# Searched priorities for three build-time schedules, a form for the sample transposes, other planned costs, and the last attention evacuations behind all products

## The chip, the cores and the metric

One core of a Trainium2 chip. Its engines run their own instruction queues and meet at semaphores: TensorE (PE; PEld is its weight load), VectorE (DVE), ScalarE (ACT), GpSimd (POOL) and SyncE (SP), which issues most DMAs. The metric is device microseconds of one execution, and what is given is the median of several runs.

## The reference

A two-layer trunk, one inference step. There are 512 new tokens of one prompt (`x_prompt`) and 8 x 4 = 32 tokens of 8 running sequences (`x_sample`), 544 rows of width 1024 in all.

```python
for i in range(DEPTH):
    h = rms_norm(x, norm_mix[i])
    if i % 2 == 0:    # conv: a*sigmoid(gate), causal depthwise conv of 31, layer norm, silu, w_out
        out, st = conformer_conv(h, conv_past[c], ...)
    else:             # stick-breaking attention, 16 heads of 64
        qkv = (h @ attn_w_qkv[a]).reshape(b, t, 3, N_HEADS, HEAD_DIM)
        att = stick_breaking_attention(q, k_all, v_all, attn_b_logit[a], past_len)
        out = att.reshape(b, t, N_HEADS * HEAD_DIM) @ attn_w_o[a]
    x = x + out
    h = rms_norm(x, norm_ffn[i])
    out, st = conv_ffn(h, ...)    # (silu(conv3(h @ w_gate)) * (h @ w_up)) @ w_down
    x = x + out
y = rms_norm(x, norm_final)
```

For the samples the keys and values of 256 past positions come from a paged cache, 2 pages of 128 rows for each sequence. The weights of attention are `exp(log_sigmoid(z) + sum over later keys of log_sigmoid(-z))`, a reversed running sum along the keys in place of a softmax. New K and V rows and the conv states are outputs too. Everything is f32.

## The kernel before, in words

**Numbers.** Each f32 product is made of three passes over split operands: x as XH + XL, a weight as whi + wlo, and XH·whi + XL·whi + XH·wlo. ScalarE makes whi from the raw weights (L397, a cast), VectorE wlo (L400, raw minus whi); a weight slot is 128 x 1024, and five split slots are in use in turn. The same holds for activations: XH by ScalarE, XL by VectorE.

**Stages, in order of time.** Conv mixer of layer 0 (to about 214.6 us): the rows come in as `xr` (128 rows each) and `xs` (the 32 sample rows), are transposed on TensorE (L998) and split to XH and XL (L1005, L1007); products with w_in at L755 to L757; depthwise taps as products of diagonals (L892); layer norm; w_out. FFN of layer 0 (to about 635): gate and up at L1401 to L1403, down at L1625 to L1627; the first products of the attention's queries lie in its end. Attention (to about 871): K and V products by 128 columns, called chunk c, at L2125 to L2127; K and V back to rows (L2155) for the outputs; pages gathered by POOL (`xT<-in_cache_k_dram`), turned (L2245) and used for sample logits (L2263, 32 columns at a time) and sample values (L2325, 32 rows); prompt logits with 64 contracted rows (L2387); exp, ln, running sum and exp on ScalarE and VectorE; the weights transposed (L2429) and multiplied by V into 64 columns (L2449, tile `av`). For chunks 0 to 6 `av` is copied whole; for chunk 7, the last, three units of products go to `av`, and each 128-column block of it is cast to XH (L2458) and subtracted to XL (L2459). Then w_o and, with an order of its own, the FFN of layer 1 and the final norm (to 1268).

**What sets the order.** No order is written out by hand. Each stage makes a list of operations of `Plan` (class at L105) with an engine, a planned cost in us, what they read and write, and the function that issues the instructions. `run` then walks planned time: for the engine that is free first it takes, among the operations whose inputs are ready about then, the one with the smallest key, and calls its function, so that all queues are filled in that order:

```python
t + CHANGE_BIAS * turn - self.eager * rank[i] - self.urgent.get(i, 0.0) -
    (STICK if self.follows.get(i, -1) == last.get(eng) else 0.0)
```

`rank` is the longest planned chain behind the operation. `urgent` holds written urgencies plus the **shifts**, a string of `index:delta` pairs, where index counts the operations of the list in the order of their making. `turn` is 0.17 us (times CHANGE_BIAS, 3) if a TensorE operation has another `form` than the one before it; None is the form of the plain 128 x 128 matmuls, "c32", "c64" and "r64" are blocks with 32 or 64 output columns or 64 contracted rows. PSUM and other buffers are handed out in the order in which operations come to use them. The conv list is `Plan(E_CONV, 0.12, CONV_SHIFTS)` (L718), FFN `Plan(E_FFN)` (L1311), attention `Plan()` (L2077). Planned costs and arrival times serve the order alone; on the chip an engine waits for what its instruction needs.

Of the kernel before, what the change touches and what calls it, by code (L numbers as in the profile page):

```python
# [14 lines left out]
ALU = mybir.AluOpType  # L15
# [234 lines left out]
def tile_trunk(  # L250
# [737 lines left out]
    def incoming(h):  # L988
# [3 lines left out]
        for j in range(NC // per):  # L992
            pt = psum(("tr", "av")[(j + 1) % 2])
            for i in range(per):
                c = j * per + i
                o = i * n
                for t, m, b in mine:
                    plan.op("pe", 0.107, lambda c=c, o=o, t=t, m=m, b=b, pt=pt: pe.transpose(  # L998
                        pt()[:, o + b * P - c0:o + b * P - c0 + m], t[:, c * P:(c + 1) * P], ident[:m, :m]),
                        r=[("x", b)], w=[pt])  # L1000
# [300 lines left out]
    def ffn(l, before, after):  # L1301
# [9 lines left out]
        plan = Plan(E_FFN)  # L1311
# [765 lines left out]
    plan = Plan()  # L2077
# [22 lines left out]
    def dcost(n):  # L2100
        return 0.09 + n * 1.1e-3

    def acost(n):
        return 0.1 + n * 0.95e-3
# [55 lines left out]
    def keys(c, h):  # L2160
        c0, n = (SA, SB)[h]
        pt = project(k0 + TURNS.index(("k", c)), h)
        plan.op("act", acost(256), lambda: act.copy(kT[:, c, c0:c0 + 256], pt()[:, :256]),  # L2163
                r=[pt], w=[("k", c, h)] + ([("ktp", i) for i in range(4)] if c >= 4 else []))
        if h:
            plan.op("act", 0.2, lambda: act.copy(kT_s[:, c, :], pt()[:, 256:n]), r=[pt], w=[("kT_s", c)])
        rows, src = to_rows(lambda b: kT[:, c, c0 + b * P:c0 + (b + 1) * P], [("k", c, h)])
        kr = sbuf("kr", 2 * P, 2)
        plan.op("dve", 0.38, lambda: dve.tensor_copy(kr().rearrange("p (b d) -> p b d", b=2), src()), r=[rows], w=[kr])
        plan.op("sp", 3.0, lambda: nc.sync.dma_start(out=kpv[:, 2 * h:2 * h + 2, c * P:(c + 1) * P],  # L2170
                                                     in_=kr().rearrange("p (b d) -> p b d", b=2)), r=[kr])

    def values(c, h):
# [4 lines left out]
        if h:  # L2178
            plan.op("act", 0.2, lambda: act.copy(vT_s[:, c, :], pt()[:, 256:n]), r=[pt], w=[("vT_s", c)])
        rows, src = to_rows(lambda b: vt()[:, b * P:(b + 1) * P], [vt])  # L2180
        plan.op("dve", 0.38, lambda: dve.tensor_copy(vtok[c % 3][:, 2 * h:2 * h + 2, :], src()),
# [23 lines left out]
    def page(i):  # L2205
# [21 lines left out]
    def page_logits(m):  # L2227
# [8 lines left out]
        for odd in range(2):  # L2236
            for pg in range(2):
                t = page(4 * m + 2 * odd + pg)
                for half in range(2):
# [7 lines left out]
                    plan.op("pe", 0.43, turn, r=[t, (t, 1), "pages"], w=[pt])  # L2247
# [6 lines left out]
                    plan.op(eng, 0.68 if half == 0 else 0.6, keep, r=[pt], w=[("ktq" if odd else "ktp", 2 * pg + half)],  # L2254
# [11 lines left out]
        plan.op("pe", 1.72, logits, r=[(k, i) for k in ("ktp", "ktq") for i in range(4)] + ["Qz", *second], w=[z], form="c32")  # L2266
        if m % 2:
            for g in range(2):
                plan.op("dve", 0.45, lambda g=g: dve.tensor_scalar(
# [3 lines left out]
    def new_logits():  # L2273
# [10 lines left out]
        plan.op("pe", 0.6, f, r=[("kT_s", c) for c in range(NC)], w=[zn], form="c32")  # L2284
        for t in range(4):
            plan.op("dve", 0.25, lambda t=t: dve.scalar_tensor_tensor(
# [3 lines left out]
    def to_columns(t, pt, src, dst, key, r):  # L2290

        plan.op("pe", 0.12, lambda: [pe.transpose(pt()[:, i * P:(i + 1) * P], x, ident) for i, x in enumerate(src)], r=r, w=[pt])
        plan.op("act", 0.12 + 0.12 * len(src), lambda: act.copy(dst, pt()[:, :len(src) * P].rearrange("p (g r) -> p g r", r=P)),
# [10 lines left out]
    def new_weights():  # L2304
# [3 lines left out]
        for i in range(4):  # L2308
            rows = slice(32 * i, 32 * i + 32)
            plan.op("act", 0.2, lambda rows=rows: act.activation(Zw[rows, :, rows], Zn[rows], AF.Exp), r=["Zn"], w=[("Zw", i)])  # L2310
# [3 lines left out]
    def sequence(n):  # L2314
# [13 lines left out]
        plan.op("pe", 0.9, f, r=[*ts, *((t, 1) for t in ts), ("wT", 2 * bg), ("wT", 2 * bg + 1), "pages"], w=[pt], form="c32")  # L2328
# [4 lines left out]
        else:  # L2333
            plan.op("dve", 0.37, lambda: dve.scalar_tensor_tensor(o, pt()[:, :2 * P], m, o, op0=ALU.mult, op1=ALU.add),
# [4 lines left out]
    def new_values(bg):  # L2339
# [19 lines left out]
        plan.op("act", 0.4, lambda: act.copy(  # L2359
# [9 lines left out]
    def pair(c):  # L2369
        av = psum("av")  # L2370

        def unit(parts):
# [17 lines left out]
            plan.op("pe", 1.69e-3 * n, logits, r=[x for cc in cs for x in (("q", cc), ("k", cc, 0), ("k", cc, 1))], w=z, form="r64")  # L2390
            for j in range(2):
                for cc, (lo, m) in cs.items():
                    plan.op("act", acost(m), lambda j=j, cc=cc, lo=lo, m=m: act.activation(
# [12 lines left out]
            plan.op("dve", 0.1 + n * 1.06e-3, lambda: dve.tensor_scalar(  # L2406
# [4 lines left out]
            for j in range(2):  # L2411
                for i, lo, _ in parts:
# [6 lines left out]
                    plan.op("dve", 0.08 + m * 2.15e-3, scan, w=[(s, j)])  # L2419
            sj = [(s, 0), (s, 1)]  # L2420
            plan.op("act", acost(2 * n), lambda: act.activation(two(s)[:, :, :n], two(s)[:, :, :n], AF.Exp, scale=-1.0), w=sj)
            plan.op("dve", 0.08 + 2 * n * 1.08e-3, lambda: dve.tensor_tensor(
                two(e)[:, :, :n], two(e)[:, :, :n], two(s)[:, :, :n], op=ALU.mult), r=sj, w=ej)
            for j in range(2):
# [6 lines left out]
                plan.op("pe", 0.82e-3 * n, turn, r=[(e, j)], w=[t])  # L2431
# [148 lines left out]
```

## Time and profile before

| | us |
|---|---|
| median of 3 runs | 1270.52 (1269.94 to 1270.71) |
| profiled execution | 1269.8 |
| span of its trace | 1268.1 |
| TensorE busy | 1257.2, 10846 matmuls |
| VectorE busy | 1004.7, 1696 instructions |
| ScalarE busy | 717.5, 1436 instructions |
| GpSimd busy | 166.0, 291 instructions |
| granted clock of TensorE | 0.998 of full speed |

A row of the timeline is: start, duration, engine, line, operation, out<-in, tile or shape, count, and in brackets the idle time before it with what ended it. A row of the waits is: engine, tile and line that waited, what it waited for, then total us, times and longest. A row of the groups is: line, engine, operation, shapes, count, then busy us and mean ns, then idle time before. A row of the windows is: stretch of time, sum of busy time of all engines that count, then busy us of PE, PEld, DVE, ACT and POOL with their counts, the granted clock, the share of DMA and GB/s. Matmuls are pipelined, so a row's duration overlaps the next row's start; the spacing of starts is what one costs.

### The profile page before, as it was taken

The numbers are of one execution on the slowest core, as the hardware profiler recorded it, in microseconds if no ns is written. First come the engines' busy times: TensorE is split into PE (matmuls) and PEld (weight loads), VectorE is DVE, ScalarE is ACT, GpSimd is POOL, SyncE is SP. The second block draws the span as 40 slices with busy tenths as digits, with TensorE's granted clock in tenths as the row PEclk, the third lists the DMA queues.
The fourth block names the chain that finished last, engine by engine and source line by source line (L and its number), as shares of the span: only waits on it lengthen the run. The fifth ranks groups of instructions, "written<-read, shape, count | busy, mean of one in ns | idle before, by whom it ended". The sixth has DMA issues, their size and how long they took to land.

```text
span 1268.1 us, 26470 instructions
## 1 busy us (share of the span) xinstructions
PE 1257.2 (99%) x10846; PEld 1207.7 (95%) x10846; DVE 1004.7 (79%) x1696; ACT 717.5 (57%) x1436; POOL 166.0 (13%) x291
## 2 busy tenths in 40 slices
PE   9999999999999999999999999999999999999998
PEld 8997699999999999999989888999999999999998
DVE  7999876979987887869865589766988987886863
ACT  7794584635655455445564598754646645455453
POOL 5000014101001000002042143200111001000000
PEclk9999999999999999999999999999999999999999
DMA  7455423133233233244354443342123233232221
GB/s 221 131 165 156 119 69 115 35 100 102 92 112 99 74 112 115 62 144 172 116 185 154 152 144 132 119 145 73 62 85 117 91 96 117 67 119 91 85 77 72
DMA packets 119179, 142.39 MB, mean 112 GB/s; under 512 B 5101, under 2 KB 110245, under 8 KB 118786
## 3 DMA queue, kind: packets, MB, share of 16 engines
q1 hardware_dynamic: 110350, 111.89, 28.2%
q0 software_dynamic: 8704, 28.80, 7.0%
q8 instruction: 85, 1.39, 0.5%
q14 instruction: 36, 0.29, 0.1%
q10 hardware_dynamic: 4, 0.01, 0.0%
HBM read 129.34 MB, written 12.18 MB: 112 GB/s over the span
## 4 chain that ended last, share of the span: by engine, by line
PE 88%; DVE 9%; ACT 1%; issue 1%; DMA 0%; DVEq 0%; ACTq 0%
PE acc L1627 5%; PE acc L1626 5%; PE acc L1625 5%; PE acc L755 4%; PE acc L756 4%; PE acc L757 4%; PE av L892 3%; PE tr L1627 3%; PE tr L1626 3%; PE tr L1625 3%; PE av L1401 3%; PE av L1402 3%; PE av L1403 3%; PE tr L1401 3%; PE tr L1402 3%; PE tr L1403 3%
## 5 line engine op out<-in xcount | busy, mean ns | idle before, releaser
L397 ACT CAST whi<-raw 128x1024 fp32r<-128x1024 f32 (+2 forms) x247 | 224.3, 912 | 122.2 <-PE av L1402 25.1
L400 DVE TENSOR_TENSOR wlo<-raw,whi 128x1024 fp32r<-128x1024 f32 (+2 forms) x247 | 259.1, 1052 | 26.6 <-ACT whi L397 24.9
L755 PE MATMUL acc<-XH,whi 128*128 128x288 f32 (+1 forms) x384 | 112.7, 294 | 0.0
L757 PE MATMUL acc<-XH,wlo 128*128 128x288 f32 (+1 forms) x384 | 110.3, 287 | 0.9 <-DVE wlo L400 0.9
L756 PE MATMUL acc<-XL,whi 128*128 128x288 f32 (+1 forms) x384 | 110.3, 287 | 0.0
L1401 PE MATMUL av<-HH,whi 128*128 128x288 f32 (+1 forms) x280 | 83.3, 298 | 0.4 <-DVE xT L1716 0.4
L1627 PE MATMUL acc<-TH,wlo 128*128 128x272 f32 x288 | 83.0, 288 | 0.0
L1626 PE MATMUL acc<-TL,whi 128*128 128x272 f32 x288 | 82.7, 287 | 0.0
L1625 PE MATMUL acc<-TH,whi 128*128 128x272 f32 x288 | 82.7, 287 | 0.0
L1402 PE MATMUL av<-HL,whi 128*128 128x288 f32 (+1 forms) x280 | 82.6, 295 | 0.0
L2125 PE MATMUL acc<-XH,whi 128*128 128x256 f32 (+1 forms) x264 | 82.0, 311 | 0.6 <-ACT kT L2163 0.6
L1403 PE MATMUL av<-HH,wlo 128*128 128x288 f32 (+1 forms) x280 | 82.3, 294 | 0.0
L1661 ACT COPY G<-acc 128x272 f32<-128x272 f32 (+1 forms) x72 | 26.8, 372 | 94.7 <-PE acc L1627 94.7
L1401 PE MATMUL tr<-HH,whi 128*128 128x256 f32 (+1 forms) x280 | 79.1, 283 | 0.0
L1402 PE MATMUL tr<-HL,whi 128*128 128x256 f32 (+1 forms) x280 | 78.9, 282 | 0.0
L1403 PE MATMUL tr<-HH,wlo 128*128 128x256 f32 (+1 forms) x280 | 78.5, 280 | 0.0
L2127 PE MATMUL acc<-XH,wlo 128*128 128x256 f32 (+1 forms) x264 | 75.8, 287 | 0.0
L2126 PE MATMUL acc<-XL,whi 128*128 128x256 f32 (+1 forms) x264 | 75.8, 287 | 0.0
L755 PEld LDWEIGHTS acc<-XH,whi 128*128 128x128 f32 x384 | 72.2, 188 | 1.4 <-issue 0.4
L757 PEld LDWEIGHTS acc<-XH,wlo 128*128 128x128 f32 x384 | 72.1, 188 | 1.1 <-DVE wlo L400 1.1
L756 PEld LDWEIGHTS acc<-XL,whi 128*128 128x128 f32 x384 | 72.2, 188 | 0.3
L1564 DVE SCALAR_TENSOR_TENSOR cv<-G,fprm,cv 128x560 f32<-128x560 f32 x88 | 69.5, 797 | 0.5
(465 smaller groups left out, 4372.7 us busy)
## 6 DMA issues: line engine op xcount, KB each, us to landing
raw<-in_ffn_w_gate_dram SPq DMA_DIRECT2D x22, 1024.0 KB
raw<-in_ffn_w_up_dram SPq DMA_DIRECT2D x22, 1024.0 KB
raw<-in_ffn_w_down_dram SPq DMA_DIRECT2D x24, 768.0 KB
raw<-in_attn_w_qkv_dram SPq DMA_DIRECT2D x12, 1024.0 KB
raw<-in_conv_w_in_dram POOLq DMA_DIRECT2D x6, 1024.0 KB, 8.7
rep<-glu SPq DMA_DIRECT2D x36, 142.0 KB
raw<-in_conv_w_out_dram POOLq DMA_DIRECT2D x4, 1024.0 KB, 7.0
raw<-in_ffn_w_down_dram SPq DMA_DIRECT2D x8, 512.0 KB
```

What stands on the lines that cost most here:

```text
L397: act.copy(hi[:, k, :], src[:, k])
L400: dve.tensor_tensor(lo[:, k, :], src[:, k], hi[:, k, :], op=ALU.subtract)
L755: pe.matmul(o, hi[:, k, :], XH[:, k, c0:c0 + n], start=(k == 0), stop=False)
L756: pe.matmul(o, hi[:, k, :], XL[:, k, c0:c0 + n], start=False, stop=False)
L757: pe.matmul(o, lo[:, k, :], XH[:, k, c0:c0 + n], start=False, stop=(k == NC - 1))
L1401: pe.matmul(o, hi[:, j + k, :], xh, start=(start and k == 0), stop=False, **kw)
L1402: pe.matmul(o, hi[:, j + k, :], xl, start=False, stop=False, **kw)
L1403: pe.matmul(o, lo[:, j + k, :], xh, start=False, stop=(stop and k == len(xs) - 1), **kw)
L1625: pe.matmul(o, hi[:, j + k, :], xh, start=(start and k == 0), stop=False, **kw)
L1626: pe.matmul(o, hi[:, j + k, :], xl, start=False, stop=False, **kw)
L1627: pe.matmul(o, lo[:, j + k, :], xh, start=False, stop=(k == 3), **kw)
L2125: pe.matmul(o, hi[:, k, :], XH[:, k, c0:c0 + n], start=(k == 0), stop=False)
```

## The change

Every product, copy and DMA stays; both kernels issue the same instructions. Five edits concern their order.

1. `CONV_SHIFTS` becomes another table of searched numbers.
2. The attention list gets such a table (`ATTN_SHIFTS`), and the FFN list gets one for layer 0 (`FFN_SHIFTS`); layer 1's has none, as before.
3. Transposes of the 32 sample rows in the conv stage have a form, "x32", so leaving and entering them is charged as a turn.
4. Many planned costs of the attention list are other numbers, and a page counts as there 5.6 us after its gather in place of 4.0.
5. For the last chunk, the casts and subtractions of `av` read all three units of products, where each had read its own.

```diff
 CONV_SHIFTS = (
-    "14:-0.3 19:-5.6 22:-0.9 26:-9.4 28:-1.2 30:-9.6 31:-6.4 37:-7.1 40:-29.6 41:-19.9 42:-3.6 46:-3.3 47:-6.6 49:-12.8 51:-6.1 "
...
+    "18:-4.8 19:2 22:-3.9 26:-6.9 32:-13 36:-14.1 38:-3.4 39:-9 40:-0.8 42:-3.2 43:-0.8 47:-6.8 48:-11.2 50:-4.7 52:-5.3 53:-3.9 "
...
+ATTN_SHIFTS = (
+    "9:0.4 10:6.7 21:19 29:4.8 35:4.5 41:5 49:2.8 50:-5.6 53:-22.8 96:-1.7 115:0.3 124:2.4 130:7.9 136:4.4 146:2.2 174:-0.2 175:-6.9 "
...
+FFN_SHIFTS = (
+    "11:0.6 13:-10.2 17:-13.3 34:-2.8 35:2.4 37:2.8 38:0.7 41:-0.4 48:-7.5 49:-6.8 55:-1.6 56:-7.6 58:7.5 60:3.2 64:-13 101:-17.8 "
...
                         pt()[:, o + b * P - c0:o + b * P - c0 + m], t[:, c * P:(c + 1) * P], ident[:m, :m]),
-                        r=[("x", b)], w=[pt])
+                        r=[("x", b)], w=[pt], form="x32" if m < P else None)
...
-        plan = Plan(E_FFN)
+        plan = Plan(E_FFN, shifts="" if l else FFN_SHIFTS)
...
-    plan = Plan()
+    plan = Plan(shifts=ATTN_SHIFTS)
     plan.change = CHANGE
...
     def dcost(n):
-        return 0.09 + n * 1.1e-3
+        return 0.05 + n * 1.045e-3
 
     def acost(n):
-        return 0.1 + n * 0.95e-3
+        return 0.035 + n * 0.9e-3
...
-            plan.op(f"page{i}", 4.0, lambda: None, r=[("asked", i)], w=[(t, 1)])
+            plan.op(f"page{i}", 5.6, lambda: None, r=[("asked", i)], w=[(t, 1)])
...
-        plan.op("pe", 1.72, logits, r=[...], w=[z], form="c32")
+        plan.op("pe", 1.695, logits, r=[...], w=[z], form="c32")
...
-            products(range(len(units)), 2.1, av)
+            products(range(len(units)), 2.165, av)
...
             for u in range(len(units)):
                 for i, _ in units[u]:
-                    out(i * P, P, lambda cols: av()[:, cols], [(av, u)], i)
+                    out(i * P, P, lambda cols: av()[:, cols], [(av, v) for v in range(len(units))], i)
```

The lines of the changed kernel are 27 higher than those of the same code before, from the tables on (L755 is L782, L998 is L1025).

**Place 1: ScalarE at the start of the program.** The rows run from its copy of the first parameters to the second half of the first weight slot; XH is the activation, whi_192 the first slot's high part (two halves of 512), ssq the sum of squares. Before:

```order
L983 COPY prm<-tr_231 128x8x4
L1005 ACTIVATE XH<-tr_240,prm 128x256
L1005 ACTIVATE XH<-av_226,prm 128x256
L1005 ACTIVATE XH<-av_224,prm 128x256 x2
L1005 ACTIVATE XH<-tr_240,prm 128x256
L1026 ACTIVATE ssq<-ssq,eps_t 128x2
L397 CAST whi_192<-raw_150 128x512
L1005 ACTIVATE XH<-tr_273,prm 128x256
L397 CAST whi_192<-raw_150 128x512
```

And of the change:

```order
L1010 COPY prm<-tr_224 128x8x4
L1032 ACTIVATE XH<-av_233,prm 128x256 x2
L1032 ACTIVATE XH<-av_235,prm 128x256 x2
L424 CAST whi_192<-raw_150 128x512
L1053 ACTIVATE ssq<-ssq,eps_t 128x2
L1032 ACTIVATE XH<-tr_265,prm 128x256 x2
L1032 ACTIVATE XH<-tr_268,prm 128x256
L424 CAST whi_192<-raw_150 128x512
```

The first half of whi stood behind five activations and the square root; now it stands behind four activations, and three activations lie between the halves instead of one.

**Place 2: TensorE in the conv stage, where the sample rows are transposed.** `xs` are the sample rows, `xr` rows of the prompt, av and tr PSUM tiles, acc a tile of products. Before, a stretch of twelve rows:

```order
L998 MATMUL tr_503<-ident,xr_109 128x128
L998 MATMUL tr_503<-ident,xr_110 128x128
L998 MATMUL tr_503<-ident,xs 128x32
L998 MATMUL tr_507<-ident,xr_109 128x128
L998 MATMUL tr_507<-ident,xr_110 128x128
L998 MATMUL tr_507<-ident,xs 128x32
L998 MATMUL av_512<-ident,xr_109 128x128
L998 MATMUL av_512<-ident,xr_110 128x128
L998 MATMUL av_512<-ident,xs 128x32
L998 MATMUL av_518<-ident,xr_109 128x128
L998 MATMUL av_518<-ident,xr_110 128x128
L998 MATMUL av_518<-ident,xs 128x32
```

And of the change, where the first of them stand:

```order
L1025 MATMUL tr_434<-ident,xr_109 128x128
L1025 MATMUL av_431<-ident,xr_110 128x128
L1025 MATMUL tr_434<-ident,xr_110 128x128
L1025 MATMUL tr_434<-ident,xs 128x32
L1025 MATMUL tr_389<-ident,xs 128x32
L1025 MATMUL av_431<-ident,xs 128x32
L1025 MATMUL av_386<-ident,xs 128x32
L782 MATMUL acc_446<-XH,whi_404 128x256
```

Four of the eight sample transposes stand together now, and the other four as one, two and one; before, three stood together and five alone.

**Place 3: ScalarE at the end of attention.** e are attention weights, Zd the samples' output, av the last chunk's tile, sqa the squares of the next norm. Before:

```order
L2458 CAST XH<-av_10518 128x128 x2
L2432 COPY e_10337<-t_10539 128x512
L2359 COPY Zd<-one_10546 128x8x32
L474 CAST XH<-Zd 64x8x32 x2
L2458 CAST XH<-av_10518 128x128 x2
L565 ACTIVATE sqa_10654<-xT 128x256
```

And of the change:

```order
L2459 COPY e_10338<-t_10555 128x512
L2386 COPY Zd<-one_10575 128x8x32
L501 CAST XH<-Zd 64x8x32 x2
L2485 CAST XH<-av_10505 128x128 x4
L592 ACTIVATE sqa_10654<-xT 128x256
```

All four casts of `av` are together behind the third unit of products. On TensorE that unit is now followed by 24 products of tile one_10587 and 18 more; before by 30 of tiles z and 12 of one_10565 with 6 more.

More of the change, by code (lines that the diff above doesn't have):

```diff
@@ L86 @@
 CONV_SHIFTS = (
[15 rows of a table removed]
[15 rows of a table added]
+)
+ATTN_SHIFTS = (
[8 rows of a table added]
+)
+FFN_SHIFTS = (
[11 rows of a table added]
 )
@@ L2165, in keys @@
         if h:
-            plan.op("act", 0.2, lambda: act.copy(kT_s[:, c, :], pt()[:, 256:n]), r=[pt], w=[("kT_s", c)])
+            plan.op("act", 0.09, lambda: act.copy(kT_s[:, c, :], pt()[:, 256:n]), r=[pt], w=[("kT_s", c)])
         rows, src = to_rows(lambda b: kT[:, c, c0 + b * P:c0 + (b + 1) * P], [("k", c, h)])
         kr = sbuf("kr", 2 * P, 2)
-        plan.op("dve", 0.38, lambda: dve.tensor_copy(kr().rearrange("p (b d) -> p b d", b=2), src()), r=[rows], w=[kr])
+        plan.op("dve", 0.33, lambda: dve.tensor_copy(kr().rearrange("p (b d) -> p b d", b=2), src()), r=[rows], w=[kr])
         plan.op("sp", 3.0, lambda: nc.sync.dma_start(out=kpv[:, 2 * h:2 * h + 2, c * P:(c + 1) * P],
@@ L2178, in values @@
         if h:
-            plan.op("act", 0.2, lambda: act.copy(vT_s[:, c, :], pt()[:, 256:n]), r=[pt], w=[("vT_s", c)])
+            plan.op("act", 0.09, lambda: act.copy(vT_s[:, c, :], pt()[:, 256:n]), r=[pt], w=[("vT_s", c)])
         rows, src = to_rows(lambda b: vt()[:, b * P:(b + 1) * P], [vt])
-        plan.op("dve", 0.38, lambda: dve.tensor_copy(vtok[c % 3][:, 2 * h:2 * h + 2, :], src()),
+        plan.op("dve", 0.33, lambda: dve.tensor_copy(vtok[c % 3][:, 2 * h:2 * h + 2, :], src()),
             r=[rows], w=[("vtok", c % 3, h)])
@@ L2252, in keep @@
                         copy(home[:, :, pg * P:(pg + 1) * P], pt().rearrange("p (c k) -> p c k", c=4))
-                    plan.op(eng, 0.68 if half == 0 else 0.6, keep, r=[pt], w=[("ktq" if odd else "ktp", 2 * pg + half)],
+                    plan.op(eng, 0.59 if half == 0 else 0.5, keep, r=[pt], w=[("ktq" if odd else "ktp", 2 * pg + half)],
                             a=[second[half]] if odd else [])
@@ L2264, in logits @@
                                   start=(b == 0 and g == 0), stop=(b == 3), skip_group_check=True)
-        plan.op("pe", 1.72, logits, r=[(k, i) for k in ("ktp", "ktq") for i in range(4)] + ["Qz", *second], w=[z], form="c32")
+        plan.op("pe", 1.695, logits, r=[(k, i) for k in ("ktp", "ktq") for i in range(4)] + ["Qz", *second], w=[z], form="c32")
         if m % 2:
             for g in range(2):
-                plan.op("dve", 0.45, lambda g=g: dve.tensor_scalar(
+                plan.op("dve", 0.395, lambda g=g: dve.tensor_scalar(
                     Zd[:, 2 * bg + g, :], z()[:, g * KW:(g + 1) * KW], bcol[:, g:g + 1], None, op0=ALU.add),
@@ L2282, in f @@
                               start=(t == 0), stop=(t == 3), skip_group_check=True)
-        plan.op("pe", 0.6, f, r=[("kT_s", c) for c in range(NC)], w=[zn], form="c32")
+        plan.op("pe", 0.22, f, r=[("kT_s", c) for c in range(NC)], w=[zn], form="c32")
         for t in range(4):
-            plan.op("dve", 0.25, lambda t=t: dve.scalar_tensor_tensor(
+            plan.op("dve", 0.16, lambda t=t: dve.scalar_tensor_tensor(
                 Zn[:, t, :], zn()[:, t * NS:(t + 1) * NS], bcol[:, t % 2:t % 2 + 1], mnew[:, t // 2, :],
@@ L2290, in to_columns @@
     def to_columns(t, pt, src, dst, key, r):
-        plan.op("pe", 0.12, lambda: [pe.transpose(pt()[:, i * P:(i + 1) * P], x, ident) for i, x in enumerate(src)], r=r, w=[pt])
-        plan.op("act", 0.12 + 0.12 * len(src), lambda: act.copy(dst, pt()[:, :len(src) * P].rearrange("p (g r) -> p g r", r=P)),
+        plan.op("pe", 0.109 * len(src), lambda: [pe.transpose(pt()[:, i * P:(i + 1) * P], x, ident) for i, x in enumerate(src)], r=r, w=[pt])
+        plan.op("act", 0.04 + 0.115 * len(src), lambda: act.copy(dst, pt()[:, :len(src) * P].rearrange("p (g r) -> p g r", r=P)),
                 r=[pt, "sd"], w=[(key, t)])
@@ L2309, in new_weights @@
             rows = slice(32 * i, 32 * i + 32)
-            plan.op("act", 0.2, lambda rows=rows: act.activation(Zw[rows, :, rows], Zn[rows], AF.Exp), r=["Zn"], w=[("Zw", i)])
+            plan.op("act", 0.1, lambda rows=rows: act.activation(Zw[rows, :, rows], Zn[rows], AF.Exp), r=["Zn"], w=[("Zw", i)])
         for t in range(0, 4, 2):
@@ L2326, in f @@
                                   ts[pg]()[:, c * P:(c + 1) * P], start=(g == pg == 0), stop=(pg == 1), skip_group_check=True)
-        plan.op("pe", 0.9, f, r=[*ts, *((t, 1) for t in ts), ("wT", 2 * bg), ("wT", 2 * bg + 1), "pages"], w=[pt], form="c32")
+        plan.op("pe", 0.84, f, r=[*ts, *((t, 1) for t in ts), ("wT", 2 * bg), ("wT", 2 * bg + 1), "pages"], w=[pt], form="c32")
         o, m = oacc[:, bg, :], own[:, b:b + 1]
@@ L2333, in sequence @@
         else:
-            plan.op("dve", 0.37, lambda: dve.scalar_tensor_tensor(o, pt()[:, :2 * P], m, o, op0=ALU.mult, op1=ALU.add),
+            plan.op("dve", 0.395, lambda: dve.scalar_tensor_tensor(o, pt()[:, :2 * P], m, o, op0=ALU.mult, op1=ALU.add),
                     r=[pt], w=[("oacc", bg)])
@@ L2358, in new_values @@
         plan.op("pe", 0.25, turn, r=[("oacc", bg)], w=[t])
-        plan.op("act", 0.4, lambda: act.copy(
+        plan.op("act", 0.275, lambda: act.copy(
             dec[:, :, 4 * bg:4 * bg + 4, :], t()[:, :2 * P].rearrange("p (c b r) -> p c b r", c=NC, b=4)),
@@ L2388, in logits @@
                                   kT[HALF[j], cc, 0:(i + 1) * P], start=(lo == 0), stop=True, skip_group_check=True)
-            plan.op("pe", 1.69e-3 * n, logits, r=[x for cc in cs for x in (("q", cc), ("k", cc, 0), ("k", cc, 1))], w=z, form="r64")
+            plan.op("pe", 1.745e-3 * n, logits, r=[x for cc in cs for x in (("q", cc), ("k", cc, 0), ("k", cc, 1))], w=z, form="r64")
             for j in range(2):
                 for cc, (lo, m) in cs.items():
-                    plan.op("act", acost(m), lambda j=j, cc=cc, lo=lo, m=m: act.activation(
+                    plan.op("act", 0.1 + acost(m), lambda j=j, cc=cc, lo=lo, m=m: act.activation(
                         two(e)[:, j, lo:lo + m], z[j]()[:, lo:lo + m], AF.Exp, bias=bb[:, 2 * cc + j:2 * cc + j + 1]),
```

10 lines of the change are left out of this document (5 added, 5 removed), and 45 rows, old and new, of tables (ATTN_SHIFTS, CONV_SHIFTS, FFN_SHIFTS).

## The prediction

> **What bounds the kernel now.** I read the page first (busy rows, slices, chain of waits), then TensorE's waits, and then its rows one by one with their start times.
>
> ```profile
> span 1268.1 us, 26470 instructions
> PE 1257.2 (99%) x10846; PEld 1207.7 (95%) x10846; DVE 1004.7 (79%) x1696; ACT 717.5 (57%) x1436; POOL 166.0 (13%) x291
> PEclk9999999999999999999999999999999999999999
> PE 88%; DVE 9%; ACT 1%; issue 1%; DMA 0%; DVEq 0%; ACTq 0%
> ```
>
> TensorE is the bound: 99% busy, 88% of the chain, at one granted clock throughout. Its waits, each with total, times and longest:
>
> ```profile
> PE warm L1049 <- DVE zero L645: 1.3, 1, 1.3
> PE acc L757 <- DVE wlo L400: 0.9, 1, 0.9
> PE acc L2125 <- ACT kT L2163: 0.6, 1, 0.6
> PE av L1401 <- ACT fprm L1223: 0.5, 1, 0.5
> PE av L1625 <- ACT qT L1865: 0.5, 1, 0.5
> PE av L1401 <- DVE xT L1716: 0.4, 2, 0.2
> PE one L2155 <- DVE kr L2169: 0.4, 1, 0.4
> PE tr L1743 <- DVE sqa L1803: 0.3, 1, 0.3
> ```
>
> These eight kinds are all it has: 1.3 + 0.9 + 0.6 + 0.5 + 0.5 + 0.4 + 0.4 + 0.3 = 4.9 us in 1268. So an order can gain in two ways only: by taking those waits away, or by making the same 10846 matmuls follow each other more closely. The second does not show in busy time, because a matmul's shown duration overlaps the next one. It shows in the starts:
>
> ```profile
> 693.14 0.60 PE L2245 MATMUL t<-ident,xT 128*128 128x128 f32 x4
> 693.50 0.36 PE L2125 MATMUL acc<-XH,whi 128*128 128x256 f32 x1
> 693.70 0.28 PE L2126 MATMUL acc<-XL,whi 128*128 128x256 f32 x1
> 693.82 0.28 PE L2127 MATMUL acc<-XH,wlo 128*128 128x256 f32 x1
> ...
> L2125 PE MATMUL acc<-XH,whi 128*128 128x288 f32 x128 | 40.8, 319 | 0.0
> L2126 PE MATMUL acc<-XL,whi 128*128 128x288 f32 x128 | 37.8, 295 | 0.0
> ```
>
> In the stream of products, starts are 0.12 apart (693.70 to 693.82). Behind four transposes the first product is followed only after 0.20 (693.50 to 693.70): coming back to the products costs 0.08 us. The two groups say the same: L2125 heads each triple and L2126 follows it, 319 against 295 ns, 24 ns x 128 = 3.1 us for this shape alone. I call such a place a **seam**.
>
> **Sample transposes (L998), priced from their rows.**
>
> ```profile
> 21.45 0.24 PE L998 MATMUL av<-ident,xs 32*128 32x32 f32 x1
> 21.53 0.28 PE L998 MATMUL tr<-ident,xs 32*128 32x32 f32 x2
> 21.74 0.38 PE L755 MATMUL acc<-XH,whi 128*128 128x256 f32 x1
> 27.55 0.38 PE L998 MATMUL tr<-ident,xr 128*128 128x128 f32 x2
> 27.86 0.24 PE L998 MATMUL tr<-ident,xs 32*128 32x32 f32 x1
> 28.04 0.33 PE L998 MATMUL tr<-ident,xr 128*128 128x128 f32 x1
> ```
>
> Ordinary transposes follow each other 0.11 apart (four last 0.60 at 693.14, two 0.38 at 27.55, and half the difference is 0.11), so the second of the pair at 27.55 starts at 27.66. The lone sample transpose then comes 0.20 later, and the ordinary one 0.18 after it: 0.38 for the visit. Beside other sample transposes it would cost 0.08 (21.45 to 21.53), and the ordinary pair around it 0.11. A lone visit therefore costs 0.38 - 0.11 - 0.08 = **0.19 us** too much. The order of before makes six visits (three transposes together, five alone), the changed order four (four together, one, two, one): 2 x 0.19 = 0.4 us. Runs of one form in the conv stage fall from 36 to 30; the other four, and the returns to products that go with them, I price at one seam each, 0.08 to 0.1: another 0.35. Conv stage: **-0.75 us**, with ends at -0.4 (visits alone) and -1.1 (all six at 0.19).
>
> [...]
>
> **Attention seams.**
>
> ```profile
> 696.40 0.29 PE L2127 MATMUL acc<-XH,wlo 128*128 128x288 f32 x1
> 696.62 1.07 PE L2263 MATMUL dz<-kT,xT 128*32 128x256 f32 x16
> 697.51 1.05 PE L2263 MATMUL dz<-e,xT 128*32 128x256 f32 x16
> 698.49 0.40 PE L2125 MATMUL acc<-XH,whi 128*128 128x288 f32 x1
> 698.73 0.29 PE L2126 MATMUL acc<-XL,whi 128*128 128x288 f32 x1
> 698.86 0.29 PE L2127 MATMUL acc<-XH,wlo 128*128 128x288 f32 x1
> ```
>
> Going into a block in another form costs 696.62 - 696.40 - 0.13 = 0.09, coming back 698.73 - 698.49 - 0.13 = 0.11. In the order of before the products are left and re-entered 72 times in this stage, in the changed order 66 times; blocks in a form of their own stand directly behind one another 14 times instead of 8. Six returns at 0.085 are 0.5 us; six places where a leave and an entry (0.2) become one direct switch, taken as half, are 0.6. Attention: **-1.1 us**, ends -0.5 and -1.7. For FFN layer 0 the same count gives two returns fewer, -0.2. The final FFN has its old order. Seams together: -0.75 - 0.2 - 1.1 = **-2.05 us**.
>
> **Waits, start of the program.**
>
> ```profile
> 10.60 0.28 PE L756 MATMUL acc<-XL,whi 128*128 128x256 f32 x1
> 11.80 0.39 PE L757 MATMUL acc<-XH,wlo 128*128 128x256 f32 x1 [0.92 <-DVE wlo L400]
> 15.68 0.38 PE L755 MATMUL acc<-XH,whi 128*128 128x256 f32 x1
> ...
> 14.36 1.21 DVE L400 TENSOR_TENSOR wlo<-raw,whi 128x1024 fp32r<-128x1024 f32 x1
> ```
>
> The third product could start at 10.60 + 0.12 = 10.72 and starts at 11.80, for it waits for the first wlo: 1.08 lost, of which the waits show 0.92; the other 0.16 is the restart, and I add it to every wait that goes. In the changed order ScalarE casts the first half of whi directly behind four XH activations, ahead of the square root and two more XH; so the first product and its wlo come earlier, about 1 us. But the second weight slot of before is ready at 14.36 + 1.21 = 15.57 and used at 15.68. Its cast still stands behind both halves and the same kind of copies, so what is gained ahead of it runs into it. Gain between 0 and 1.08; I take 0.25, the nearest to the end that the 15.57 row gives.
>
> **Waits, conv and FFN.** VectorE is nearly full here, so an order tuned closer has little air:
>
> ```profile
> 50.00:100.00 50.00, 50.00 (x406) 50.00 (x406) 47.46 (x87) 46.59 (x181) 3.54 (x4) 1.00 0.51 149
> ```
>
> 47.46 of 50 us busy on VectorE, 46.59 on ScalarE, and yet TensorE waits nowhere. The new table keeps all of that work and permutes it. Around the first layer norm the changed order leaves TensorE and VectorE within some tenths of a us of each other, around the second it leaves some 2 us. The wait for fprm (0.5) stands on rows that do not change, so it stays. I take 0 here, with ends -0.9 (two of the FFN waits, 0.5 and 0.3 on L1625 and L1743, gone with 0.1 of seam) and +3: at a VectorE that is 95% busy, one evacuation a weight split late is 1.2 us (the 14.36 row), and two or three such are the end I allow.
>
> **Waits, attention.** Two waits (0.6 on kT, 0.4 on kr) may go, since the two were on copies whose planned cost is changed; with their restarts 1.2 us. Against them stands a new one: ahead of the transposes for the last but one group of weights (L2429 by the old lines) I find VectorE's product ready 0.2 to 0.3 us after TensorE gets there. Pages are not waited for in any of the rows of waits; that the planner now takes 5.6 us for them can only move the gathers ahead, and their landing takes
>
> ```profile
> xT<-in_cache_k_dram,idx POOLq DMA_INDIRECT x14, 6.1
> ```
>
> 6.1 us, still above the planned 5.6, so a tight page would be 0.5 us late, and there are 32. I take 0 for attention's waits in sum, ends -1.2 and +2.
>
> **Last evacuations.**
>
> ```profile
> 839.48 0.39 PE L2125 MATMUL z<-XH,whi 128*128 128x256 f32 x1
> 839.59 0.43 ACT L2458 CAST XH<-av 128x128 fp32r<-128x128 f32 x2 [2.36 <-PE av L2449]
> 840.06 0.49 DVE L2459 TENSOR_TENSOR XL<-av,XH 128x128 fp32r<-128x128 f32 x2 [2.36 <-ACT XH L2458]
> ```
>
> Before, two of the four casts and subtractions stand behind the third unit of products; the changed order puts all four there. The chain behind the unit was 840.06 + 0.49 - 839.48 = 1.07 us and becomes two more subtractions longer, 0.49: 1.56. It hides behind the products that do not need chunk 7: 18 of them stand directly behind the unit, 18 x 0.118 = 2.1 us. Cover remains with 0.5 us to spare; if it were gone, the whole cost would be 1.56. It removes nothing that TensorE waited for. I cost it at 0.
>
> **Sum.** Span 1268.1, profiled execution 1269.8: 1269.8 - 2.05 - 0.25 + 0.25 (the new wait) = 1267.75. The median of the runs, 1270.52, lies 0.7 above the profiled one; as a median I predict **1268.4 us**, -0.17%.
>
> **Rivals.** (B) The waits go as well: the kT, kr, qT and sqa waits (0.6 + 0.4 + 0.5 + 0.3 and 0.16 of restart each) and most of the 0.9 at the start. That is up to 3.3 us beyond the seams; taken at two thirds, 1266.2. For it: each sits on a line whose order changes. Against it: the start is held by the second slot. Chance 0.30. (C) The change does not do what it says: seams are only traded, or the 2 us are handed to two or three new waits of the size that before has (0.4 to 0.9): 1270.4. For it: the order of before had been arranged as closely, and eight waits were left all the same. [...] Chance 0.22. (D) Slower: VectorE in the conv stage. It has 2.5 us of air in the 50 us quoted; if a wlo (1.2 us) stands one place later than the product that needs it, four times, 4 x 1.2 = 4.8, less the seams: 1273.3. It decides from the fourth such wait, because 2.05 + 2.54 (0.2% of the time, about what a measurement of this kernel can tell from no change) is 4.6. Nothing in the rows of before shows one in that stretch. Chance 0.12. My forecast itself: 0.36.
>
> **How the numbers follow.** Unknown ends: seams -3.0 to -0.9, start -1.1 to 0, FFN and conv waits -0.9 to +3, attention waits -1.2 to +2. They do not all fall together; 8 times in 10 I expect 1265.2 to 1272.0. Faster by over 0.2% means under 1267.98: most of B and a third of the forecast, 0.42. Slower means over 1273.06: most of D and a little of C, 0.10. Within: 0.48.
>
> **What would show it.** Right, if the groups L2125 and L2126 (27 lines further down) come closer than 24 ns, visits of sample transposes show four seams of 0.2, TensorE's waits sum to 4 to 6 us, and the wait ahead of the first wlo is shorter while the second slot starts at 15.3 to 15.7. Wrong, if the waits sum to more than 8 us or under 3; a wait on XH or XL behind the last av unit would break the cover that I claim, and a wait on a page the term for attention. Off in size only, if the stage boundaries (F's first product at 214.6, attention's at 635, the end of av at 839.5) shift by other amounts than 1.0, 0.2 and 1.1.

## The result and the profile after

The changed kernel takes 1272.78 us in the median of 22 runs (1270.47 to 1275.24), the one before 1270.51 (1269.41 to 1270.92): a ratio of 1.0022, interval [1.0016, 1.0028]. It is slower by 0.2%, and its runs spread over 4.8 us where those of before spread over 1.5. Forecast were 1268.4 us and a range of 1265.2 to 1272.0.

The page of the changed kernel (profiled execution 1274.86 us) answers line by line to the one of before:

```profile
span 1273.1 us, 26466 instructions
PE 1261.0 (99%) x10846; PEld 1211.9 (95%) x10846; DVE 1001.2 (79%) x1696; ACT 717.7 (56%) x1436; POOL 172.6 (14%) x291
PEclk9999989999999999999999999999999999999999
PE 85%; DVE 9%; DMA 2%; ACT 2%; issue 1%; POOL 0%; SPq 0%; DVEq 0%; ACTq 0%; POOLq 0%
```

TensorE is as full as before and waits little longer by its share, but two things are new: DMA is in the chain (2%), and one of the forty digits of the granted clock is an 8. TensorE's waits name the place:

```profile
PE av L1247 <- DMA prod<-in_state_ffn_dram: 2.4, 1, 2.4
PE warm L1076 <- DVE zero L672: 1.3, 1, 1.3
PE tr L1062 <- DVE XL L1034: 0.8, 1, 0.8
PE av L1652 <- ACT qT L1892: 0.5, 1, 0.5
PE av L1428 <- ACT fprm L1250: 0.4, 1, 0.4
PE av L1428 <- DVE xT L1743: 0.2, 1, 0.2
PE acc L784 <- DVE wlo L427: 0.2, 1, 0.2
PE one L2182 <- DVE kr L2196: 0.2, 1, 0.2
```

Against the list of before, the waits on kT (0.6) and sqa (0.3) are gone, those on wlo, kr and xT shorter, and two are new: 2.4 us for a load of FFN rows, and 0.8 us for a VectorE copy. The eight add up to 6.0 us, against 4.9 before: the sum hardly moved, though this execution is 5 us longer. Around the first of them the timeline of TensorE reads:

```profile
181.83 0.28 PE L784 MATMUL acc<-XH,wlo 128*128 128x256 f32 x1
184.55 1.04 PE L1247 MATMUL av<-ident,prod 40*128 40x40 f32 x8 [2.44 <-DMA prod<-in_state_ffn_dram]
185.52 0.58 PE L782 MATMUL acc<-XH,whi 128*128 128x256 f32 x1
185.90 0.41 PE L783 MATMUL acc<-XL,whi 128*128 128x256 f32 x1
186.12 0.41 PE L784 MATMUL acc<-XH,wlo 128*128 128x256 f32 x1
186.33 0.41 PE L782 MATMUL acc<-XH,whi 128*128 128x256 f32 x1
```

Behind the wait the starts of products are 0.21 us apart (186.12 to 186.33), not 0.12. The windows of the same stretch show the clock (the third figure from the end is the granted clock):

```profile
175.00:181.10 6.10, 6.10 (x51) 5.94 (x50) 4.11 (x6) 3.15 (x7) 2.29 (x3) 1.00 0.52 149
181.10:184.50 3.40, 1.01 (x9) 0.81 (x7) 3.40 (x10) 3.37 (x8) 0.00 (x0) 1.00 0.65 176
184.50:187.90 3.40, 3.35 (x19) 3.31 (x20) 0.66 (x2) 1.85 (x5) 1.55 (x2) 0.50 0.15 41
187.90:191.30 3.40, 3.40 (x18) 3.40 (x18) 0.25 (x1) 0.00 (x0) 0.00 (x0) 0.50 0.00 0
191.30:195.00 3.70, 3.70 (x32) 3.70 (x32) 3.02 (x7) 3.22 (x9) 0.73 (x1) 0.99 0.00 0
```

From 184.5 to 191.3 the clock is 0.50: 18 or 19 matmuls pass in 3.4 us where, at 0.118 us apart, 29 would, and TensorE counts as wholly busy all the while. The wait of 2.4 us cost its own length, and the half clock that follows it nearly half of 6.8 us again.

**Where the time went.** From the starts of the matmuls I take each stage's length from its first matmul to the next stage's first, and split off the waits (what a matmul that waited starts later than the median of the same two neighbours without a wait); the half clock stays in the rest. All in us:

| stage | before: length (waits, rest) | after | difference |
|---|---|---|---|
| start, to the 25th conv product | 15.68 | 16.46 | +0.78 |
| conv, from there | 198.90 (0.57, 198.32) | 204.87 (3.88, 200.99) | +5.97 |
| FFN layer 0 | 418.93 (1.44, 417.49) | 418.25 (1.02, 417.23) | -0.68 |
| attention | 211.73 (1.72, 210.01) | 210.63 (0.35, 210.28) | -1.10 |
| w_o, FFN layer 1, end | 416.82 (0.54, 416.28) | 416.89 (0.53, 416.36) | +0.07 |

The whole loss is in the conv stage and the start; all that lies behind them is 1.7 us shorter. The start is partly chance, as shown at the end. The table is of one execution, 1274.86 us long, 2.1 above the median of its kernel: between the profiles lie 5.0 us, between the medians 2.3.

**Why the load was late.** SyncE's issues in the changed kernel, up to the loads that TensorE waits for:

```profile
175.86 0.68 SPq L1204 DMA_DIRECT2D out_dram<-prod  x1
176.71 0.34 SPq L1238 DMA_DIRECT2D prod<-in_ffn_w_dw_dram  x1
177.24 0.42 SPq L387 DMA_DIRECT2D raw<-in_ffn_w_up_dram  x1
177.70 0.43 SPq L1239 DMA_DIRECT2D prod<-in_ffn_b_dw_dram  x1
178.17 0.32 SPq L1240 DMA_DIRECT2D prod<-in_state_ffn_dram  x1
```

The last of three small loads is issued at 178.17, behind a weight tile of 1 MB (raw13, L387). In the trace's DMA packets, 1024 packets of 1 KB start from 178.3 on and end at 182.4. Of the 80 packets of 4 KB of the small loads six start by 177.92, the others only from 181.6 on, and the last ends at 184.02; TensorE goes on at 184.55. In the kernel before, raw13 was issued at 171.54, far ahead of the small loads, and the tile that follows (raw14) is issued behind them:

```profile
194.43 0.32 SPq L1213 DMA_DIRECT2D prod<-in_state_ffn_dram  x1
...
196.21 0.40 SPq L360 DMA_DIRECT2D raw<-in_ffn_w_gate_dram  x1
...
199.45 0.68 PE L1220 MATMUL av<-ident,prod 40*128 40x40 f32 x8
```

There the small packets are through at 197.24, and TensorE turns them only at 199.45.

### The profile page after: what moved, and what is told of

It is laid out like the page before. It is cut to its first block, busy times and chain, and to the rows that moved or that the text cites. A ratio compares the mean times of both kernels' runs of the same rounds, so it can differ in the third digit from the quotient of the medians.

```text
span 1273.1 us, 26466 instructions
## 1 busy us (share of the span) xinstructions
PE 1261.0 (99%) x10846; PEld 1211.9 (95%) x10846; DVE 1001.2 (79%) x1696; ACT 717.7 (56%) x1436; POOL 172.6 (14%) x291
## 4 chain that ended last, share of the span: by engine, by line
PE 85%; DVE 9%; DMA 2%; ACT 2%; issue 1%; POOL 0%; SPq 0%; DVEq 0%; ACTq 0%; POOLq 0%
PE acc L1654 5%; PE acc L1653 5%; PE acc L1652 5%; PE av L1428 3%; PE tr L1654 3%; PE tr L1652 3%; PE tr L1653 3%; PE av L1429 3%; PE av L1430 3%; PE acc L782 3%; PE acc L783 3%; PE acc L784 3%; PE tr L1428 3%; PE tr L1429 3%; PE tr L1430 3%; PE av L919 3%
## 5 line engine op out<-in xcount | busy, mean ns | idle before, releaser
L782 PE MATMUL acc<-XH,whi 128*128 128x288 f32 (+1 forms) x384 | 114.3, 298 | 0.0
L2152 PE MATMUL acc<-XH,whi 128*128 128x256 f32 (+1 forms) x264 | 81.3, 308 | 0.0
L782 PEld LDWEIGHTS acc<-XH,whi 128*128 128x128 f32 x384 | 73.4, 191 | 1.5 <-issue 0.4
```

The source lines that it names most:

```text
L782: pe.matmul(o, hi[:, k, :], XH[:, k, c0:c0 + n], start=(k == 0), stop=False)
L2152: pe.matmul(o, hi[:, k, :], XH[:, k, c0:c0 + n], start=(k == 0), stop=False)
```

## The experiments

Ratios are to the kernel before, run on the same chip with them; its median was 1270.47 us beside e1 to e4, 1269.95 beside e5 to e8 and 1270.32 beside e9 to e12.

**e1: the conv edits alone, on the kernel before.**

```diff
 CONV_SHIFTS = (
-    "14:-0.3 19:-5.6 22:-0.9 26:-9.4 ...
+    "18:-4.8 19:2 22:-3.9 26:-6.9 ...
-                        r=[("x", b)], w=[pt])
+                        r=[("x", b)], w=[pt], form="x32" if m < P else None)
```

> The kernel before with the two conv edits alone (the new conv table and the form of the sample transposes). Theory: all of the loss is made in the conv stage. In the two profiled runs the first product of FFN layer 0 comes at 221.33 in place of 214.57 us, +6.75, of which 2.6 us are a wait for a DMA of FFN rows at 184.5, 2.7 us the half clock behind it and 1.0 us a wait at 36.0. The profiled run of the changed kernel lies 2.1 us above its median, so I expect a median of 1270.5 + 6.75 - 2.1 = 1275 us, first FFN product at 219 to 222. Rival: the loss comes from the attention or FFN tables, or from conv and attention together; then 1270.5 or less here, and no wait on a DMA.

1273.61 us (1271.25 to 1275.46), ratio 1.0029 [1.0018, 1.0039]: slower, as expected, by 1.4 us less than the 1275 that I had set. In its profile the conv stage has 4.05 us of waits, FFN and attention the lengths of before (418.88 and 211.68). This profile has the same wait, 1.4 us long, and no half clock behind it; the first FFN product comes at 217.69, below the 219 to 222 that I expected. Without the half clock the conv stage outside waits is 197.74 us: 0.58 less than before, and 3.25 less than in the profile above, which is thus the price of the half clock.

**e2: everything but the conv edits.** (The reverse of that diff, on the changed kernel.)

> The changed kernel with the two conv edits undone. Theory: what the other edits brought in the profile stays, -0.7 us in FFN layer 0 and -1.1 in attention: 1270.5 - 1.8 = 1268.7 us, with a spread of the runs as narrow as before's (1.5 us). Rival: attention or FFN costs too, then 1270.5 or more.

1268.74 us (1267.71 to 1269.86), 0.9987 [0.9978, 0.9996], spread 2.15 us. All of the loss is made by the conv edits. The waits that are left:

```profile
PE warm L1076 <- DVE zero L672: 1.3, 1, 1.3
PE acc L784 <- DVE wlo L427: 0.9, 1, 0.9
PE av L1428 <- ACT fprm L1250: 0.5, 1, 0.5
PE av L1652 <- ACT qT L1892: 0.5, 1, 0.5
PE av L1428 <- DVE xT L1743: 0.2, 1, 0.2
```

kT, kr and sqa are not among them. Attention takes 210.50 us, with 0.28 of waits and 210.22 outside: against 211.73, 1.72 and 210.01 before. So the gain in attention is waits, all of it; outside waits the stage became 0.2 us longer, not 1.1 shorter.

**e3, e5, e6: TensorE works through the wait.** On the changed kernel, ahead of the first transposes of FFN rows; e6 is e3 again, for another profile.

```diff
+            if f0 == 0:
+                for _ in range(21):      # e3, e6
+                    pe.transpose(pt()[:, 0:P], ident, ident)
...
+                for _ in range(20):      # e5 in their place
+                    pe.matmul(pt()[:, 0:2 * P], XH[:, 0, 0:P], XH[:, 0, 0:2 * P], start=True, stop=True)
```

> The changed kernel with 21 transposes of the identity (0.109 us each, 2.3 us) ahead of the first transposes of the FFN rows, into the PSUM tile that these overwrite. TensorE works through the wait. Theory: the granted clock falls because TensorE stood idle; filled, the products behind it stay 0.118 us apart in place of 0.213 and the first FFN product comes 2.7 us earlier; median 1272.8 - 2.5 = 1270.3. Rival: the clock falls for another cause (the burst of the DMA, the form of the transposes); then the products stay 0.213 apart and the time 1272.8.

1274.29 us (1270.66 to 1274.96): not 1270.3. Three runs had a clock of 0.999 and 1270.7 to 1272.0, four 0.995 to 0.997 and 1274.3 to 1275.0. The profile is of the first kind: the wait is filled, no half clock follows it, span 1269.4. But the median is no lower than the changed kernel's 1272.78, so the lower clock of the other four (0.995 to 0.997) must come from another place or from something else.

> As the kernel with the wait filled by transposes, but filled with 20 products (128x256 of the split activations, 0.118 us each, 2.36 us) whose result is overwritten. With transposes four of seven runs still showed a granted clock of 0.995 to 0.997 and 1274.3 to 1275.0 us, the other three 0.999 and 1270.7 to 1272.0. Theory 1: the clock falls after a stretch with too little work at 182 to 185 us, and transposes do not count as work; then no run here is under 0.998 and the median is 1271. Theory 2: in those runs the clock falls at another place, after the wait at 36 us; then the same mixture comes again, with a median between 1271 and 1274. Rival: real work there changes nothing, 1272.8 and the spread of the changed kernel.

1271.75 us (1270.59 to 1274.03), 1.0018 [1.0009, 1.0027]: seven of eleven runs at 1270.6 to 1271.9, four at 1273.2 to 1274.0. Fewer at the longer time, yet the mixture is there with real products too. For theory 2, not against it. The clock alone doesn't sort the runs, though: of the four, two have 0.995 and 0.997, two 0.998.

> The kernel filled with transposes once more, for one more profile. If the run is one with a clock of 0.995 to 0.997, its trace shows where the half clock lies: behind 182 to 185 us (theory 1), behind the wait at 36 us (theory 2), or at the start of the program alone, where the clock opened at 4.74 us in the profile of before and at 5.77 to 7.02 in the others. In a run with 0.999 it shows none but the start.

1275.05 us, clock 0.995, and the profile shows the place:

```profile
34.87 0.29 PE L784 MATMUL acc<-XH,wlo 128*128 128x288 f32 x1
37.19 0.58 PE L1062 MATMUL tr<-dg,mean_m 128*128 128x128 f32 x1 [2.02 <-DVE XL L1034]
```

and in its windows:

```profile
30.00:36.00 6.00, 4.87 (x34) 3.95 (x32) 5.48 (x11) 5.23 (x18) 0.00 (x0) 1.00 0.47 146
36.00:42.80 6.80, 5.61 (x22) 5.33 (x23) 4.68 (x12) 2.63 (x10) 0.00 (x0) 0.50 0.30 75
```

In this run the other new wait, at 35 us, lasted 2.0 us, and the half clock stands there, 36.0 to 42.8; behind the filled place, as in the profiles of e3 and e5, there is none. For this run theory 2 holds. Why four of seven runs of e3 had a clock under 0.998 and 1274.3 us or more, although its order up to 36 us is that of the changed kernel, stays open. That wait, too, begins with a DMA that lands late. In the changed kernel's profile:

```profile
28.07 1.05 ACT L424 CAST whi<-raw 128x1024 fp32r<-128x1024 f32 x1 [1.44 <-DMA raw<-in_conv_w_in_dram]
...
29.15 1.23 DVE L427 TENSOR_TENSOR wlo<-raw,whi 128x1024 fp32r<-128x1024 f32 x1 [1.65 <-ACT whi L424]
31.91 3.60 DVE L866 SCALAR_TENSOR_TENSOR dwh<-ext_p,prm,dwh 128x256 f32<-128x256 f32 x7
35.42 0.51 DVE L1034 SCALAR_TENSOR_TENSOR XL<-tr,prm,XH 128x288 fp32r<-128x288 f32 x1
```

ScalarE waits for raw2; behind it VectorE's wlo, then seven tap sums that stand in the queue ahead of the copy (L1034) which frees the PSUM tile for TensorE's L1062. In e6 the cast came at 29.26, 1.2 us later than here, and TensorE 1.2 us later.

**e4: raw12 and raw13 off SyncE's queue. e7: besides, raw2 and raw3 onto it.** Both on the changed kernel; no order changes but that of the loads.

```diff
-CONV_RAWS = 12
+CONV_RAWS = 14
...
-            (pool if self.nraw < CONV_RAWS else nc.sync).dma_start(out=t[:, :nk, :], in_=src)
+            (pool if self.nraw < CONV_RAWS and self.nraw not in (2, 3) else nc.sync).dma_start(...)   # e7 alone
```

> The changed kernel with the loads of two 1 MB weight tiles (raw12 and raw13) issued from GpSimd's queue, as those before them are, in place of SyncE's. Theory: the small loads of the FFN rows land late because 1024 packets of raw13 lie between the first and the second of them on SyncE's queue; off that queue the wait at 184.5 is under 0.5 us, no half clock follows, and the median is 1272.8 - 4.5 = 1268.3 us. Rival 1: they land late because SyncE issues them late, behind eight stores that take it 7 us; then the wait stays near 2 us and the time at 1272 to 1273. Rival 2: the 16 DMA engines are full with raw13 whichever queue it is on; then the wait stays at 1 us or more.

1269.51 us (1268.43 to 1273.49), 0.9997 [0.9988, 1.0006]. The wait for FFN rows is gone. Raw13 is issued at 172.90 now, the small packets end at 179.71, and TensorE turns the rows at 181.51 without a pause. SyncE's eight stores stand ahead of the small loads as before, so rival 1 falls; rival 2 isn't wholly excluded, since raw13 now starts 4 us earlier and is through at 178.2. The median is 1.2 us above what I expected; the profile still waits 0.8 us for XL at 35, and four runs of eleven have a clock of 0.996 or 0.997.

> The kernel with raw12 and raw13 on GpSimd's queue, and besides raw2 and raw3 on SyncE's, which is empty then, in place of GpSimd's, which issues them at 20.8 us behind its small loads although their buffer is free from 16.3. Theory: the wait of 0.75 to 1.3 us at 36 comes from raw2, which lands at 27 to 28 us where the order needs it at 25.3; it lands before 25 now, the wait is under 0.2 us and the first FFN product 0.9 us earlier; no run under a clock of 0.998 if that wait is the other cause of the half clock; median 1268.3. Rival: VectorE is late there by its own load; then the wait stays and the time is 1269.5.

1267.94 us (1267.23 to 1269.62), 0.9985 [0.9976, 0.9994], no run under a clock of 0.998. ScalarE's cast comes at 26.12 with no wait for raw2, and L1062 at 34.62 directly behind the product ahead of it. What TensorE still waits for:

```profile
PE warm L1076 <- DVE zero L672: 1.3, 1, 1.3
PE av L1025 <- DMA xr<-in_x_prompt_dram: 0.8, 1, 0.8
PE av L1652 <- ACT qT L1892: 0.5, 1, 0.5
PE av L1428 <- ACT fprm L1250: 0.4, 1, 0.4
PE acc L784 <- DVE wlo L427: 0.2, 1, 0.2
PE av L1428 <- DVE xT L1743: 0.2, 1, 0.2
```

The conv stage takes 198.27 us, against 198.90 before and 204.87 in the changed kernel. This version is faster than both kernels. Since its order is that of the changed kernel, loads apart, both new waits came from where the loads were queued, and with them went the clocks under 0.998.

**e9: the same moves of loads on the kernel before.**

> The kernel before, its order unchanged, with the same two edits of loads that brought the changed kernel to 1267.94 us (raw2 and raw3 on SyncE's queue, raw12 and raw13 on GpSimd's). It waits for neither load, so if the gain there was the change with its waits taken away, nothing happens here: within 1 us of before. Rival: the queues themselves are the better ones whatever the order; then 1268 here too.

1270.19 us, 0.9999 [0.9990, 1.0009]; all of its stages within 0.1 us of before. The queues are no better in themselves. They take away a loss that only the new order has.

**e8: attention with the new planned costs but without its table,** on e2's kernel (`plan = Plan()` in place of `Plan(shifts=ATTN_SHIFTS)`).

> The changed kernel with the conv edits undone (1268.74 us) and without the attention table, so that the new planned costs, the page time and the evacuations act alone in attention. In that kernel's profile attention takes 210.38 us against 211.73 before, and almost all of the difference are the waits on kT and kr (0.72 and 0.55 with their restarts), which are gone; the time outside waits is 210.1 against 210.0. Theory: the waits go because the copies are planned truly, so they stay away here: 1268.7 to 1269.2. Rival: the table searched them away; then waits of about 1.3 us come back, 1270.0.

1276.90 us, 1.0056 [1.0042, 1.0070]: some 8 us slower than with the table, and my theory is wrong. Attention takes 219.13 us in place of 210.50. New waits stand in it, and not those of before; those listed add up to 4.1 us, and the rest of the 8.6 was not broken down. The three longest:

```profile
PE t L2456 <- ACT e L2459: 2.3, 5, 1.0
...
PE one L2182 <- DVE vtok L2208: 0.7, 1, 0.7
PE t L2456 <- ACT XH L2485: 0.7, 1, 0.7
```

The new costs alone give a worse order; with the table the order has few waits. Whether a table searched with the old costs would have found one as good was not tried.

**e10: the last evacuations read their own unit again,** on e7's kernel (the last edit of the change reversed).

> The kernel with both loads moved (1267.94 us against 1269.95 of before), and the last evacuations of attention reading their own unit again; nothing else in the order changes but where two casts and two subtractions stand. Forecast of the evacuations: 0, since 18 products cover them. So the ratio to before stays at 0.9985 +- 0.0007 and the stretch from attention's first product to the first of w_o keeps its length within 0.1 us. Rival: two casts earlier on ScalarE push the copies of the attention weights back, 0.4 us longer; or the chain behind the last unit was not covered, then it is up to 1.5 us shorter.

1268.29 us, 0.9985 [0.9976, 0.9994]. Attention takes 210.71 us against 210.57 in e7, so the edit is worth 0.1 us, about the forecast 0; neither of the rivals' 0.4 and 1.5 is there.

**e11: the FFN table alone. e12: the form of the sample transposes alone.** Both on the kernel before, each with its edit of the change and nothing else.

> The kernel before with the FFN table alone. In the profiles FFN layer 0 went from 418.93 to 418.0 us, by waits on xT and sqa that are gone (0.38 and 0.49 with restarts). Theory: the same here, -0.8 us, 1269.2 to 1269.8 where before is 1270 to 1270.5, and no such waits in the trace. Rival: the gain hangs on the other tables; then 0.

1270.16 us, 1.0000 [0.9991, 1.0009]. The stage is 0.68 us shorter in the profile (418.25 against 418.93), as in the changed kernel, and the wait on sqa is gone; the runs' median shows only 0.16 of it, less than they can tell, and lies outside the 1269.2 to 1269.8 that I expected. By time alone the rival, 0, can't be told from it.

> The kernel before with the form of the sample transposes alone; its old conv table was searched without that form and meets another planner. Forecast by visits and seams alone: -0.2 to -0.4 us. Rival, which I hold for likelier after the runs so far: a table fits one planner only, and waits of 1 us or more come in the conv stage: 1271 to 1275.

1269.86 us, 0.9996 [0.9987, 1.0005], not clear of noise; the reading goes by the profile. No new wait in the conv stage, so the rival falls. Conv outside waits is 197.74 us against 198.32: -0.58, the same as with the new table and the form together in e1. Sample transposes make four visits there, too.

## Why the prediction was wrong, point by point

- **The step that failed** is "Waits, conv and FFN", where I took 0 and asked only whether VectorE could keep up. The reason was named as "one evacuation a weight split late". The conv stage had 3.3 us of new waits (3.88 against 0.57); with 0.4 less in FFN layer 0 the term came out at +2.9, just inside the end of +3 that I had set, but by another cause: both new waits come from loads, raw2 landing behind what the order needs, and FFN rows behind raw13. I had compared the queues of instructions for the engines and not asked of each new place on TensorE when its load is issued and what lies ahead of it on that queue. In e4 and e7 the waits go when only the queue of the loads is changed; that the loads cause them is shown.
- **The half clock** was in none of my sums, and it is the part that lies beyond the term's end. A wait was priced at its length and a restart of 0.16. In the profiled run the clock cost another 3.25 us. It makes much of the spread of the runs: the one run of the changed kernel at 0.999 took 1270.47 us, the seven at 0.995 or 0.996 took 1273.4 to 1275.2. It does not make all of it, for four runs at 0.998 lie between 1270.7 and 1273.1. All runs of e7 have 0.998 or more, as have those of the kernel before beside the experiments, and they spread over 2.4 us and under 2.
- **The signs** that I had set missed it. "TensorE's waits sum to 4 to 6 us" was met with 6.0, since waits that went elsewhere hid the new ones and the half clock is not a wait. What did show it was the stage boundary: the first FFN product moved from 214.57 to 221.33 us, where I had named a shift of 1.0.
- **Sample transposes and conv seams**: -0.75 forecast, -0.58 found (e1, e12), with four visits as counted. Inside the ends that I had set. In e12 the form alone gives all of it, with 33 runs of one form between the 37 of before and the 31 of e1 (my count from the traces, from the 25th product on): the visits paid, and the 0.35 that I had put on the other seams did not show.
- **Start**: 0.25 forecast. In the changed kernel the wait for the first wlo fell from 0.9 to 0.2 us, yet the 25th product came at 16.46 us, not between 15.3 and 15.7, because the clock opened later in that run (at 7.02 us, against 4.74 in the profile of before; see the end). Runs with about the same opening give the gain: e1 (5.77 us) reaches that product at 15.90, e11 with the conv order of before (5.75) at 16.32, but e8, also with that order (5.65), at 16.06. So 0.2 to 0.4 us are gained: about right in size, though no single run shows it.
- **FFN**: -0.2 for seams was right (417.49 to 417.23), and another 0.4 came from the waits on xT and sqa, of which rival B had named the second.
- **Attention**: the seams were forecast at -1.10 and the stage came out at -1.10, which is luck. Seams gave +0.2 to +0.3, waits -1.4, where I had taken 0 for the waits with an end of -1.2; the new wait of 0.25 that I had added did not come. The step that failed is the direct switch between blocks of other forms, taken at half of leaving and entering. In the trace of before it takes 0.20 us from the last matmul of 128 columns to the first of the next block (742.44 to 742.64, 64 output columns to 64 contracted rows), as much as going from plain transposes into such a block (L2429 to L2449, 0.20) or back (0.20). My counts were off too: by the shapes in the traces there are 12 direct switches before and 14 after, not 8 and 14. The number of runs of one form was 71 both times, and the time outside waits stayed within 0.3 us (210.01 before, 210.28 after). The row for coming back to products is true (L2125, now L2152, still needs 21 to 22 ns more than its follower):

```profile
L2152 PE MATMUL acc<-XH,whi 128*128 128x288 f32 x128 | 40.4, 316 | 0.0
L2153 PE MATMUL acc<-XL,whi 128*128 128x288 f32 x128 | 37.7, 295 | 0.0
```

  3 ns less, 0.4 us in 128: fewer returns did pay (69 in the trace, 74 before). What took it back was not broken down.
- **Pages and last evacuations**: no wait on either; both right at 0, the second with other numbers than mine. The chain behind the last unit took 2.30 us (845.16 to 847.46), not 1.56, because the casts of the samples' output stand ahead of it, and outlasted the 2.1 us of the 18 products; the first product that reads the last XL starts at 847.85, 0.4 us later.
- **Rival B** (waits go as well) is in part what happened behind the conv stage: kT and sqa went, kr halved, qT stayed. **Rival D** had the right sign and the right stage, but the mechanism was loads and clock, not four late weight splits.
- **Without the load waits** (e7) the change gains 0.15%, close to the -0.17% forecast. That is luck as well: seams were to bring -2.05 us and brought about -0.6 (conv -0.58, FFN -0.26, attention +0.27); the rest are waits that I had taken at 0.

## What to carry to other kernels

An order that was searched against planned arrival times can use up the air in front of a load. For each place where such an order moves work forward, look up when its load is issued, what was put on that queue ahead of it, and how long that takes to land; here one load of 1 MB between two small ones cost 2.6 us of waiting and 3.25 us of half clock in the profiled run, and moving two pairs of loads to other queues turned a loss of 0.2% into a gain of 0.15%. Do not judge by the sum of waits alone: here it went from 4.9 to 6.0 us while the profiled execution became 5 us longer, and the clock's price stands in no wait. When a switch between two forms is priced, take it from a row of that switch; at half the price of two others it was wrong.

## What the runs showed of the hardware

- In the fourteen traces the stretches between two changes of the granted clock last 6.83, 30.72, 177.49, 1078.61, 1225.38, 1256.11, 1259.52, 1262.93 or 1266.35 us; the last four of these lengths lie 3.41 or 3.42 us apart, and the half clock in mid-kernel lasted 6.83 us both times. It began at 184.51 us in the changed kernel, near the end of a wait of 2.44 us, and at 36.00 in e6, inside one of 2.02; waits of 1.3 and 1.4 us (both in e1) had no half clock in them or behind them.
- In e6 the clock fell only 0.84 us after the last product's shown end at 35.16. The 3.41 us ahead of that fall (32.59 to 36.00) hold 1.5 us of transposes, with gaps, and six products. What decides whether the clock falls was not settled: by shown busy time these 3.41 us hold 2.29 us, and the stretch from 33.07 to 36.49 in e1 holds 2.09 without a fall behind it.
- The clock opened at 4.74 us in the profile of before, at 7.02 in the changed kernel's and at 3.98 to 6.63 in the others. In the profile of before the warm-up matmuls start 0.21 us apart up to 4.69 us and 0.11 apart from 4.83 on. The start of the program moved with it: with the conv order of before, the 25th product comes at 15.25 us in e12 (opened at 3.98), 15.68 in before (4.74) and 16.56 in e2 (6.63). That a part of the run-to-run spread comes from this is my estimate from these three and was not measured run by run.
